# A streaming log-sum-exp: four heads' bias on GpSimd, and one multiply and one sum per tile on VectorE, a tile later

## The chip, the cores and the metric

The kernel runs on one core of a Trainium2 chip. The metric is the time of one execution in microseconds (us). All runs quoted here agree within 0.3%. Times are medians.

## The reference

```python
def reference(x, bias):          # x: 8 x 2048 x 2048 f32, bias: 8 heads x 256
    x_heads = x.reshape(B, S, H, Dh).transpose(0, 2, 1, 3)
    x_heads = x_heads + bias[None, :, None, :]
    x_tiled = np.repeat(x_heads, 2, axis=2)
    mx = x_tiled.max(axis=-1, keepdims=True)
    return mx.squeeze(-1) + np.log(np.exp(x_tiled - mx).sum(axis=-1))   # 8 x 8 x 4096
```

For each row of 2048 numbers and each of the 8 heads the kernel needs the logarithm of the sum of exp(x + bias) over the head's 256 numbers. The kernel reads 134 MB and writes 1 MB. It leaves the maximum out. The outputs are right.

## The kernel before

x is cut into 64 tiles of 128 partitions x 2 rows x 2048 numbers, 2 MB each. Nine tile buffers are loaded in a ring. A streamed tile's eight heads are treated in three ways:

- heads 0 and 1: TensorE adds the bias into PSUM (identity matmul plus ones times bias), ScalarE takes exp and sums with its accumulator;
- heads 2 to 4: GpSimd adds the bias, ScalarE takes exp, VectorE sums three heads of both rows in one reduce, one tile later;
- heads 5 to 7: ScalarE takes exp of the raw numbers; VectorE multiplies by exp(bias) (in PSUM, `w_rep`) and sums in one instruction per head and row, six a tile ("weigh"). The trace shows each as two instructions, the custom operation and an accumulator read.

```python
for t in range(T):
    ...
    if left >= NLATE:                       # all but the last two tiles
        got = add_bias([xt[:, k, 0:CPE] for k in range(K)])
        g_add(t)                            # GpSimd, heads 2..4
        w0 = CPE + NG * Dh
        exp_inplace(xt[:, :, w0:D])         # heads 5..7
        if t:
            exp_inplace(g_part(t - 1))      # heads 2..4 of the tile before
        for k in range(K):
            sum_biased(got[k], ...)         # heads 0, 1
        for k in range(K):
            for c in range(w0, D, Dh):
                weigh(xt[:, k, c : c + Dh], c // Dh, sum_at(k, c // Dh))
        if t:
            g_sum(t - 1)
    # ... the last two tiles in pieces, without GpSimd: six weighs a row (cut)
    if left == NLATE:
        exp_inplace(g_part(t)); g_sum(t)
    if 0 < t and t - 1 + NBUF < T:
        load(t - 1 + NBUF)                  # reuses the buffer of tile t - 1
```

Tile 61 is the last streamed one; 62 and 63 are the late tiles.

The softmax here doesn't subtract the row's maximum and nothing guards it: scores larger than these inputs give would overflow.

## Time and profile before

The time is 337.84 us (337.63 to 338.28, 4 runs); the profiled span is 336.1 us.

| what | before | read from |
|---|---|---|
| loads in flight | 428 GB/s from 20 to 300 us | stretches of the span |
| busiest engine | ScalarE, 89% of the span | busy times |
| GpSimd, one tile | 3.45 us | groups |
| VectorE, one tile | six weighs at 0.34 us, a reduce of 1.75 | groups, timeline |
| issue to landing of a load | 34.3 us | DMA issues |

The first lines of the page of the kernel before, busy time of the engines, and the DMA rows of the 40 slices (tenths of busy time, GB/s):

```profile
PE 235.5 (70%) x410; PEld 69.4 (21%) x410; DVE 244.6 (73%) x856; ACT 300.6 (89%) x660; POOL 224.2 (67%) x84
...
DMA  8999999999999999999999999999999999999910
GB/s 297 427 431 435 421 429 425 437 423 426 425 432 425 435 422 431 427 430 424 430 426 425 431 427 430 422 429 433 429 426 429 424 427 431 423 435 416 365 43 16
```

No engine is saturated (ScalarE, the busiest, has 89% of the span) and the DMA queues are (busy share 1.01 from 20 to 300 us), until about 319 us. The page's account of the chain that ended last, shares of the span by engine, says the same:

```profile
DMA 71%; DVE 6%; ACT 5%; PE 1%; issue 1%; SPq 0%; ACTq 0%; DVEq 0%
```

The page's DMA queues (packets, MB, share of the 16 DMA engines' span) hold a detail that becomes important below: q14 and q8 carry instructions, not data. The line under the dots is from the page's DMA issues, a load's size and its median time in us from issue to landing.

```profile
q1 hardware_dynamic: 10832, 135.17, 95.1%
...
q14 instruction: 15, 0.12, 0.1%
q8 instruction: 3, 0.05, 0.1%
...
xt<-in_x_dram SPq DMA_DIRECT2D x62, 2048.0 KB, 34.3
```

The groups of instructions (line, engine, operation, out<-in, forms, count; busy us and mean ns of one; idle before them):

```profile
L182 POOL TENSOR_TENSOR xt<-xt,b_rep 128x1536 f32<-128x1536 f32 x62 | 213.8, 3449 | 95.6 <-DMA xt<-in_x_dram 89.6
...
L200 DVE CUSTOM_DVE_ANT_0 junk<-xt,w_rep 128x256 f32<-128x256 f32 x396 | 140.4, 417 | 86.5 <-ACT xt L194 86.5
L194 ACT ACTIVATE xt<-xt 128x1536 f32<-128x1536 f32 (+1 forms) x132 | 183.4, 1435 | 13.5 <-DMA xt<-in_x_dram 12.5
L186 DVE TENSOR_REDUCE R<-xt 128x6 f32<-128x1536 f32 x62 | 108.4, 1749 | 0.7 <-ACT xt L194 0.7
```

The end of the span, from the timeline (start us, duration us, engine, line, operation). The last GpSimd add starts 0.13 us after tile 61 has landed, so it marks that moment:

```profile
315.27 3.46 POOL L182 TENSOR_TENSOR xt<-xt,b_rep 128x1536 f32<-128x1536 f32 x1 [1.46 <-DMA xt<-in_x_dram]
...
319.76 2.84 ACT L194 ACTIVATE xt<-xt 128x1536 f32<-128x1536 f32 x2
...
321.27 1.75 DVE L186 TENSOR_REDUCE R<-xt 128x6 f32<-128x1536 f32 x1 [0.73 <-ACT xt L194]
...
322.94 0.41 DVE L200 CUSTOM_DVE_ANT_0 junk<-xt,w_rep 128x256 f32<-128x256 f32 x1
...
332.25 0.42 DVE L200 CUSTOM_DVE_ANT_0 junk<-xt,w_rep 128x256 f32<-128x256 f32 x1
...
333.15 0.37 ACT L229 ACTIVATE res<-tpair 8x256 f32<-8x256 f32 x1 [0.93 <-PE tpair L216]
```

From tile 61's landing to the end there are 20.8 us (336.1 - 315.3); call it the tail. Pieces of tiles 62 and 63 still land in it, but after 315.5 neither ScalarE nor VectorE waits for a load. The first late weigh starts at 322.94 and the last at 332.25.

### The profile page before, as it was taken

How to read it: one execution, taken by the hardware profiler on the slowest of the kernel's cores; microseconds unless marked ns; L12 is line 12 of the kernel's file. 1: busy time of each engine (PE TensorE's matmuls, PEld its weight loads, DVE VectorE, ACT ScalarE, POOL GpSimd, SP SyncE). 2: the span in 40 equal slices, each digit the busy share in tenths (PEclk: the TensorE clock that was granted, in tenths of full speed). 3: DMA queues.
4: the chain of work that ended last, by engine and by line, in shares of the span. 5: the costliest groups of instructions: out<-in, count | busy, mean ns of one | idle time of the engine just before them, and what ended most of it. 6: DMA issues, size and time to landing. Idle time of an engine off the chain costs nothing.

```text
span 336.1 us, 2806 instructions
## 1 busy us (share of the span) xinstructions
PE 235.5 (70%) x410; PEld 69.4 (21%) x410; DVE 244.6 (73%) x856; ACT 300.6 (89%) x660; POOL 224.2 (67%) x84
## 2 busy tenths in 40 slices
PE   5297785977766669767679586566894967665861
PEld 2022221222221122212122122121221212121210
DVE  0238888888878768778868777778777777877794
ACT  1469999999999989999989999899998999998995
POOL 6866766766766766766766776666775776675704
PEclk9998967596789856896765977789559596789876
DMA  8999999999999999999999999999999999999910
GB/s 297 427 431 435 421 429 425 437 423 426 425 432 425 435 422 431 427 430 424 430 426 425 431 427 430 422 429 433 429 426 429 424 427 431 423 435 416 365 43 16
DMA packets 11204, 135.46 MB, mean 403 GB/s; under 512 B 1577, under 2 KB 1849, under 8 KB 2993
## 3 DMA queue, kind: packets, MB, share of 16 engines
q1 hardware_dynamic: 10832, 135.17, 95.1%
q0 software_dynamic: 352, 0.10, 0.2%
q14 instruction: 15, 0.12, 0.1%
q8 instruction: 3, 0.05, 0.1%
q10 hardware_dynamic: 2, 0.01, 0.0%
HBM read 134.23 MB, written 1.05 MB: 402 GB/s over the span
## 4 chain that ended last, share of the span: by engine, by line
DMA 71%; DVE 6%; ACT 5%; PE 1%; issue 1%; SPq 0%; ACTq 0%; DVEq 0%
DMA xt<-in_x_dram 71%; ACT xt L194 4%; DVE junk L200 3%; DVE R L186 2%; ACT ps L165 1%; PE ps L159 1%; ACT res L229 0%; PE tpair L216 0%; DVE Rz L200 0%; DVE R L200 0%; SPq L95 0%; ACTq L194 0%; DVEq L356 0%
## 5 line engine op out<-in xcount | busy, mean ns | idle before, releaser
L182 POOL TENSOR_TENSOR xt<-xt,b_rep 128x1536 f32<-128x1536 f32 x62 | 213.8, 3449 | 95.6 <-DMA xt<-in_x_dram 89.6
L159 PE MATMUL ps<-xt,ident 128*128 128x512 f32 x256 | 183.1, 854 | 71.4 <-DMA xt<-in_x_dram 71.1
L200 DVE CUSTOM_DVE_ANT_0 junk<-xt,w_rep 128x256 f32<-128x256 f32 x396 | 140.4, 417 | 86.5 <-ACT xt L194 86.5
L194 ACT ACTIVATE xt<-xt 128x1536 f32<-128x1536 f32 (+1 forms) x132 | 183.4, 1435 | 13.5 <-DMA xt<-in_x_dram 12.5
L186 DVE TENSOR_REDUCE R<-xt 128x6 f32<-128x1536 f32 x62 | 108.4, 1749 | 0.7 <-ACT xt L194 0.7
L165 ACT ACTIVATE ps<-ps 128x256 f32<-128x256 f32 x256 | 94.6, 369 | 10.5 <-PE ps L159 6.3
L159 PEld LDWEIGHTS ps<-xt,ident 128*128 128x128 f32 x256 | 57.4, 248 | 160.3 <-DMA xt<-in_x_dram 105.1
L154 PE MATMUL ps<-b,ones 3*128 3x512 bf16 x128 | 48.7, 454 | 14.5 <-ACT ps L165 7.9
L165 ACT ACTIVATION_READ_ACCUMULATOR ps<-ps 128x1 f32 x256 | 48.5, 190 | 0.0
L200 DVE DVE_READ_ACCUMULATOR2_ANT R<- 128x1 f32 x372 | 30.6, 82 | 0.0
L154 PEld LDWEIGHTS <-ones 3*128 3x128 bf16 x128 | 7.9, 96 | 81.0 <-issue 72.7
L250 POOL DMA_DIRECT2D out_dram<-res x8 | 4.0, 505 | 9.2 <-ACT res L229 9.2
L132 PE MATMUL w_rep<-brow,ones 1*128 1x512 f32 x6 | 5.5, 1078 | 3.5 <-DMA brow<-in_bias_dram 3.5
L139 ACT ACTIVATE b_rep<-w_rep 128x768 f32<-128x768 f32 x1 | 0.8, 810 | 6.9 <-PE w_rep L132 6.9
L229 ACT ACTIVATE res<-tpair 64x512 f32<-64x512 f32 (+3 forms) x11 | 5.9, 539 | 1.2 <-PE tpair L216 0.9
L216 PE MATMUL tpair<-ident,R 128*64 128x128 f32 (+1 forms) x16 | 3.6, 310 | 2.0 <-DVE R L186 2.0
L216 PEld LDWEIGHTS tpair<-ident,R 128*64 128x64 f32 (+1 forms) x16 | 2.0, 130 | 9.1 <-DVE R L186 3.9
L216 PE MATMUL tpair<-ident,Rz 128*8 128x128 f32 x2 | 0.6, 322 | 4.4 <-DVE Rz L200 4.4
L132 PEld LDWEIGHTS w_rep<-brow,ones 1*128 1x128 f32 x6 | 1.8, 323 | 5.5 <-issue 5.5
L121 POOL CAST bparts<-brow 1x512 bf16<-1x512 f32 x1 | 0.6, 599 | 2.1 <-DMA brow<-in_bias_dram 2.1
L105 ACT ACT_TABLE_LOAD x1 | 1.3, 1283 | 0.7 <-PEq L345 0.7
L142 ACT ACTIVATE w_rep<-w_rep 128x512 f32<-128x512 f32 x3 | 1.7, 582 | 0.1
(18 smaller groups left out, 8.9 us busy)
## 6 DMA issues: line engine op xcount, KB each, us to landing
xt<-in_x_dram SPq DMA_DIRECT2D x62, 2048.0 KB, 34.3
xt<-in_x_dram SPq DMA_DIRECT2D x2, 1024.0 KB, 31.6
xt<-in_x_dram SPq DMA_DIRECT2D x2, 512.0 KB
out_dram<-res SPq DMA_DIRECT2D x7, 128.0 KB, 34.2
xt<-in_x_dram SPq DMA_DIRECT2D x3, 256.0 KB, 16.9
xt<-in_x_dram SPq DMA_DIRECT2D x2, 128.0 KB, 8.6
out_dram<-res POOLq DMA_DIRECT2D x8, 12.0 KB, 1.7
b<-bparts POOLq DMA_DIRECT2D x3, 1.0 KB, 5.7
```

The source lines that it names most:

```text
L132: nc.tensor.matmul(w_rep[:, c : c + MM], lhsT=ones, rhs=brow[:, CPE + c : CPE + c + MM], start=True, stop=True,)
L142: nc.scalar.activation(out=w, in_=w, func=ACT.Exp)
L154: nc.tensor.matmul(p[:, 0:CPE], lhsT=ones3, rhs=b3, start=True, stop=False)
L159: nc.tensor.matmul(p[:, 0:CPE], lhsT=ident, rhs=v, start=False, stop=True)
L165: nc.scalar.activation(out=p[:, c : c + Dh], in_=p[:, c : c + Dh], func=ACT.Exp, accum_out=dst(h),)
L182: nc.gpsimd.tensor_tensor(out=g_part(t), in0=g_part(t), in1=b_tile, op=ALU.add)
L186: nc.vector.tensor_reduce(out=R[b][:, :, NPE : NPE + NG, blk], in_=g_part(t).rearrange("p k (h j) -> p k h j", j=Dh), op=ALU.add, axis=myb ...
L194: nc.scalar.activation(out=v, in_=v, func=ACT.Exp)
L200: nc.vector.tensor_tensor_reduce(out=j, in0=v, in1=w_rep[:, c : c + Dh], scale=1.0, scalar=0.0, op0=ALU.mult, op1=ALU.add, accum_out=dst,)
L216: nc.tensor.transpose(out=tps[i][0:nr, k], in_=src(k), identity=ident)
L229: nc.scalar.activation(out=rv, in_=tv, func=ACT.Ln)
L250: engine.dma_start(out=ov, in_=iv)
```

## The change

GpSimd now adds the bias of four heads. ScalarE takes exp of all six heads (2 to 7) of a tile in one instruction, one tile later. VectorE multiplies heads 6 and 7 by exp(bias) in one instruction and sums all six in one reduce. Per tile that replaces six weighs and a reduce by two instructions. The late tiles are as they were.

```diff
-NG = 3
+CG = 1024
 ...
-    nc.scalar.activation(out=b_rep, in_=w_rep[:, 0 : NG * Dh], func=ACT.Copy)
+    nc.scalar.activation(out=b_rep, in_=w_rep[:, 0 : CG], func=ACT.Copy)
 ...
     def g_add(t):
-        nc.gpsimd.tensor_tensor(out=g_part(t), in0=g_part(t), in1=b_tile, op=ALU.add)
+        v = xts[t % NBUF][:, :, CPE : CPE + CG]
+        nc.gpsimd.tensor_tensor(out=v, in0=v, in1=b_tile, op=ALU.add)
-    def g_sum(t):
+    def exp_and_sum(t):
         b, blk = divmod(t, NBLK)
+        v = xts[t % NBUF][:, :, CPE:D]
+        exp_inplace(v)
+        f = v[:, :, CG:CW]
+        nc.vector.tensor_tensor(out=f, in0=f, in1=w_tile, op=ALU.mult)
         nc.vector.tensor_reduce(
-            out=R[b][:, :, NPE : NPE + NG, blk],
-            in_=g_part(t).rearrange("p k (h j) -> p k h j", j=Dh),
+            out=R[b][:, :, NPE:H, blk],
+            in_=v.rearrange("p k (h j) -> p k h j", j=Dh),
             op=ALU.add, axis=mybir.AxisListType.X)
 ...
             got = add_bias([xt[:, k, 0:CPE] for k in range(K)])
             g_add(t)
-            w0 = CPE + NG * Dh
-            exp_inplace(xt[:, :, w0:D])
-            if t:
-                exp_inplace(g_part(t - 1))
+        if 0 < t and left >= NLATE - 1:
+            exp_and_sum(t - 1)
+        if left >= NLATE:
             for k in range(K):
                 sum_biased(got[k], lambda h: sum_at(k, h))
-            for k in range(K):
-                for c in range(w0, D, Dh):
-                    weigh(xt[:, k, c : c + Dh], c // Dh, sum_at(k, c // Dh))
-            if t:
-                g_sum(t - 1)
 ...
-        if left == NLATE:
-            exp_inplace(g_part(t))
-            g_sum(t)
```

## The prediction

> **What bounds it now.** The loads. The windows from 20 to 300 us show a DMA share of 1.01 and 426 to 429 GB/s. The chain of waits is 71% DMA into xt. In the timeline one 2 MB tile lands every 4.89 us (199.00, 203.90, 208.79; about 5.05 on average). Every engine does a tile in less: ACT 4.5 to 4.7 us, DVE about 3.8 (six weigh instructions at a pitch of 0.34, one reduce of 1.75), GpSimd 3.45. Loads take 34 us to land, about seven tiles deep.
> The last tile has landed near 319.7 us, but the span is 336.1: the last 16 us are an ACT chain (exp of tile 61's GpSimd part at 319.76, then the late pieces without a gap to 330), then DVE's last weigh, ending 332.68, then 3.4 us of logarithm and output.
>
> **Costs of the change, per tile.**
> - GpSimd: 2048 instead of 1536 elements; 3.45 us scaled: 4.60.
> - DVE: drops six weighs (about 2.05 us) for one 1024-element multiply. [...]
> - ACT: one exp of 3072 for two of 1536. From 0.615 us at 512 and 1.474 at 1536: 2.76 against 2.86 for the pair.
> - Contention: GpSimd adds are 3.42 to 3.47 us whether DVE overlaps or not. The multiply's second input stays in PSUM. [...]so I add nothing.
>
> **Critical path.** All three stay under 4.89 us, GpSimd with only 0.25 to 0.3 to spare. A tile is released about 7.2 us after its successor lands instead of 5.4; the load queue shrinks from 34 to about 32 us and stays full. The stream should cost 0.
>
> The tail pays. Tile 61 lands at 315.2; its add ends at 319.9 instead of 318.7; the exp of all six heads ends at 322.6 instead of 321.2, so ACT's late pieces shift by 1.4 us. DVE then does multiply and reduce until about 327.1, and the late tiles' 24 weighs (8.2 us at 0.342) start there instead of at 322.9: last weigh ends at about 335.3 instead of 332.7. DVE, not ACT, limits the tail: +2.7 us.
>
> **Prediction: 340.4 us**, 8 in 10 between 339.2 and 342.4; faster by over 2%: 0.01, within 2%: 0.94, slower by over 2%: 0.05.
>
> **What would show it.** Groups of lines: add 4.6 us x62, multiply 1.2, reduce 3.35, exp 2.76. Busy: GpSimd near 295 us, DVE near 290, ACT a little lower (about 295). Timeline: tiles landing every 4.89 us, last load near 320 as before; time to landing 31 to 33 us. Chain of waits: at the end a run of DVE weighs from about 327 without gaps in place of ACT exps.
>
> **What would make it wrong.** GpSimd over 4.85 us (contention): it would set the pace, each 0.1 us over costing 6 us in all, and the loads would show gaps. ACT waiting for GpSimd each tile. A tail where the logarithms' transposes, waiting for DVE, stall ACT too: another 0.5 to 1 us. Or the tail hiding part, if ACT's start of tile 61 comes earlier than I think.

VectorE's terms of the sum were estimates: 1.22 us for the multiply and 3.35 for the reduce, which waits for it, together 4.6 us a tile (0.8 more than before); measured later, 1.218 and 3.355. In the tail they bring VectorE from the end of the exp at 322.6 to about 327.1; the sum came to +2.7 us, 340.4 us.

## The result, and the profile after

The changed kernel takes 337.89 us (337.77 to 338.01, 4 runs) against 337.84 (337.63 to 338.28, 4 runs): the ratio is 1.0, with a 95% interval of 0.9982 to 1.0017. (A ratio is the mean time of one kernel's runs over that of the other's of the same rounds, so not quite the ratio of the quoted medians.) The predicted 340.4 us, range 339.2 to 342.4, was too high.

The groups of the changed kernel (the last line is from the list that keeps shapes apart):

```profile
L186 POOL TENSOR_TENSOR xt<-xt,b_rep 128x2048 f32<-128x2048 f32 x62 | 281.2, 4537 | 26.2 <-DMA xt<-in_x_dram 23.8
...
L194 DVE TENSOR_REDUCE R<-xt 128x12 f32<-128x3072 f32 x62 | 208.0, 3355 | 7.2 <-DVE xt L193 1.0
...
L193 DVE TENSOR_TENSOR xt<-xt,w_rep 128x1024 f32<-128x1024 f32 x62 | 75.5, 1218 | 34.3 <-ACT xt L202 34.1
...
L202 ACT ACTIVATE xt<-xt 128x3072 f32<-128x3072 f32 x62 | 171.1, 2760 | 10.2 <-POOL xt L186 9.8
```

Every duration is close to the forecast: add 4.54 us (4.60), reduce 3.355 (3.35), multiply 1.218 (1.22), exp 2.760 (2.76). Busy times too, while the DMA rows of the slices hardly differ:

```profile
PE 236.6 (70%) x410; PEld 69.5 (21%) x410; DVE 290.2 (86%) x174; ACT 296.1 (88%) x598; POOL 291.6 (87%) x84
...
DMA  7999999999999999999999999999999999999900
GB/s 296 430 427 435 429 424 427 433 423 427 428 425 430 433 423 430 425 428 431 424 433 421 429 427 425 434 432 423 425 430 427 433 427 426 427 429 418 386 23 16
```

The end of the span in the timeline of the changed kernel:

```profile
312.17 4.54 POOL L186 TENSOR_TENSOR xt<-xt,b_rep 128x2048 f32<-128x2048 f32 x1 [0.35 <-DMA xt<-in_x_dram]
...
319.54 1.22 DVE L193 TENSOR_TENSOR xt<-xt,w_rep 128x1024 f32<-128x1024 f32 x1 [0.22 <-ACT xt L202]
...
320.86 3.35 DVE L194 TENSOR_REDUCE R<-xt 128x12 f32<-128x3072 f32 x1
...
324.13 0.41 DVE L208 CUSTOM_DVE_ANT_0 junk<-xt,w_rep 128x256 f32<-128x256 f32 x1
...
331.99 0.42 DVE L208 CUSTOM_DVE_ANT_0 junk<-xt,w_rep 128x256 f32<-128x256 f32 x1
...
332.88 0.37 ACT L237 ACTIVATE res<-tpair 8x256 f32<-8x256 f32 x1 [1.25 <-PE tpair L224]
```

The tail is there as predicted: from the last add to the end of the span it is now 23.7 us (335.9 - 312.2) instead of 20.8, that is +2.9 for a predicted +2.7, and VectorE's late weighs run from 324.13 to 332.4 without a gap. But tile 61 landed 3.1 us earlier, at 312.2 instead of 315.3. So two effects of about 3 us cancel, -3.1 and +2.9, and one of them was not in the prediction. That they nearly cancel is luck; the spans, 335.9 and 336.1, show the small rest. The same bytes, at the same GB/s, and yet the last tiles arrive sooner. Among the DMA queues of the page (and, last, its line of the loads) one line changed:

```profile
q1 hardware_dynamic: 10832, 135.17, 95.1%
...
q8 instruction: 3, 0.05, 0.1%
q14 instruction: 10, 0.08, 0.1%
...
xt<-in_x_dram SPq DMA_DIRECT2D x62, 2048.0 KB, 32.0
```

Ten packets of instructions instead of 15. They are a thousandth of the DMA time. In the trace each load raises its semaphore in 16 steps, which are read here as one from each of the 16 DMA engines, and the work on a tile starts after the 16th: tile 61's add comes 0.13 us after it. The trace keeps the times of these steps. Here are, for some loads, the first, the third and second from the end, and the last step, in us (read from the trace's completion records, not a view of the page):

```
kernel   tile    first   14th   15th   16th   16th - first
before      1    12.72  13.36  13.53  13.61    0.89
before     17    90.82  92.05  92.98  93.32    2.50
before     29   150.09 152.06 152.30 153.68    3.59
before     45   228.94 231.15 232.34 234.30    5.36
before     61   307.80 310.12 311.85 315.14    7.34
after       1    13.05  13.46  13.52  13.58    0.53
after      17    91.15  91.77  92.16  93.20    2.05
after      29   150.41 151.63 152.11 152.56    2.15
after      45   229.26 230.98 231.50 232.43    3.17
after      61   308.12 310.31 310.43 312.01    3.89
```

The first of the steps comes at the same time in both kernels, within 0.4 us. What differs is how far the last step, so the slowest DMA engine, trails. In the kernel before its lag grows from 120 us on in jumps of about 1 us, one every 45 us. (Before that it grows by 0.5, 0.8 and 0.3 us; the 0.8 shows at 73.55, after a packet of q8, of 16 KB and 1.10 us, at 71.42.) The 8 KB packets of q14 that come just before the jumps, and the landing in which each jump shows:

```
before   packet at   122.53   167.82   212.8    258.59   308.18
         jump seen   124.02   169.31   214.64   260.08   310.24
         size of it    1.03     1.01     1.03     1.05     0.96
```

In the kernel before VectorE runs some 14 instructions a tile, waits included. In the changed kernel it has 312 instructions in the trace instead of 932, and the trace has five 8 KB packets fewer. (ScalarE has 48 fewer and SyncE 55 more, which nearly cancel.) By an estimate from these counts, 620 / 5, one packet goes with some 124 of VectorE's instructions; at 14 a tile that is nine tiles' worth, or about 45 us: the spacing of the jumps. The estimate is rough, since packets are counted whole.

### The profile page after: what moved, and what is told of

Same layout as the page of the kernel before. It is cut to its first block, busy times and chain, and to the rows that moved or that the text cites. A ratio compares the mean times of both kernels' runs of the same rounds, so it can differ in the third digit from the quotient of the medians.

```text
span 335.9 us, 2193 instructions
## 1 busy us (share of the span) xinstructions
PE 236.6 (70%) x410; PEld 69.5 (21%) x410; DVE 290.2 (86%) x174; ACT 296.1 (88%) x598; POOL 291.6 (87%) x84
## 5 line engine op out<-in xcount | busy, mean ns | idle before, releaser
L186 POOL TENSOR_TENSOR xt<-xt,b_rep 128x2048 f32<-128x2048 f32 x62 | 281.2, 4537 | 26.2 <-DMA xt<-in_x_dram 23.8
L194 DVE TENSOR_REDUCE R<-xt 128x12 f32<-128x3072 f32 x62 | 208.0, 3355 | 7.2 <-DVE xt L193 1.0
L202 ACT ACTIVATE xt<-xt 128x3072 f32<-128x3072 f32 (+3 forms) x70 | 177.5, 2539 | 10.2 <-POOL xt L186 9.8
L193 DVE TENSOR_TENSOR xt<-xt,w_rep 128x1024 f32<-128x1024 f32 x62 | 75.5, 1218 | 34.3 <-ACT xt L202 34.1
L154 PE MATMUL ps<-b,ones 3*128 3x512 bf16 x128 | 48.0, 450 | 12.6 <-DMA b<-bparts 6.5
L224 PE MATMUL tpair<-ident,R 128*64 128x128 f32 (+1 forms) x16 | 4.3, 367 | 10.0 <-DVE R L194 10.0
L208 DVE CUSTOM_DVE_ANT_0 junk<-xt,w_rep 128x256 f32<-128x256 f32 x24 | 8.3, 416 | 0.0
L139 ACT ACTIVATE b_rep<-w_rep 128x1024 f32<-128x1024 f32 x1 | 1.0, 1025 | 6.9 <-PE w_rep L132 6.9
```

The lines of the kernel that those rows point to most:

```text
L154: nc.tensor.matmul(p[:, 0:CPE], lhsT=ones3, rhs=b3, start=True, stop=False)
L186: nc.gpsimd.tensor_tensor(out=v, in0=v, in1=b_tile, op=ALU.add)
L193: nc.vector.tensor_tensor(out=f, in0=f, in1=w_tile, op=ALU.mult)
L194: nc.vector.tensor_reduce(out=R[b][:, :, NPE:H, blk], in_=v.rearrange("p k (h j) -> p k h j", j=Dh), op=ALU.add, axis=mybir.AxisListType.X,)
L202: nc.scalar.activation(out=v, in_=v, func=ACT.Exp)
L208: nc.vector.tensor_tensor_reduce(out=j, in0=v, in1=w_rep[:, c : c + Dh], scale=1.0, scalar=0.0, op0=ALU.mult, op1=ALU.add, accum_out=dst,)
```

## The experiments

The kernel before ran beside each experiment on the same chip: 337.91 us (7 runs) beside e1 to e4, 337.77 (9 runs) beside e5 to e7.

The theory, F, is a guess to be tested, for no trace shows the path of a packet: each engine's instructions are fetched by DMA packets that go through one of the 16 DMA engines; each packet sets that one back by about 1 us in a stream that never pauses, and nothing catches up. A load lands when the slowest has delivered. The change saved five of VectorE's packets and with that 3.1 us, which paid for the longer tail.

Rival Q: the changed kernel frees its buffers later, so its load queue is shorter (32.0 us to landing instead of 34.3), and that is what makes the stream end earlier. Rival W: the weighs themselves, their work or their writes, slowed the loads. A third doubt concerns the tail: whether its cost is real and what it is worth.

"Lag" below is the distance of the last from the first of the 16 steps for tile 61.

### More instructions on VectorE, in the kernel before (e1_before_nop_dve)

```diff
+NFILL = 10
 ...
             if t:
                 g_sum(t - 1)
+            for _ in range(NFILL):
+                nc.vector.engine_nop()
```

> The kernel before, with ten do-nothing engine instructions added on VectorE at the end of each streamed tile (620 in all), where VectorE is idle anyway. Theory F (instruction fetch): VectorE's instructions are fetched in 8 KB packets, and each packet sets one of the 16 DMA engines back by about 1 us; 620 more instructions [...]are about 5 more packets, so the last of the 16 completions of a load trails the first by about 12 us at the end instead of 7.3, tile 61 lands near 320 instead of 315.2, and the time is about 342.5 us (+4.8). Rival Q (the earlier landing in the changed kernel came from later buffer release and a shorter load queue): no more lag, time 337.9. Rival W (it came from the absence of the weighs' own work or of their writes): 337.9. If VectorE became the limit instead, its busy share would be above 95% and the load slices would show gaps.

Measured: 342.14 us (341.98 to 342.25), ratio 1.0124 (1.0107 to 1.0141). A filler takes about 14 ns in the trace and VectorE's busy time stays at 244.7 us. The lag is 11.72 us, tile 61's last step comes at 319.43, and its first at 307.71, where it always was. The tail is 20.9 us, unchanged. The instruction queue of this run's page, and its last add in the timeline:

```profile
q14 instruction: 20, 0.16, 0.1%
```

```profile
319.57 3.46 POOL L183 TENSOR_TENSOR xt<-xt,b_rep 128x1536 f32<-128x1536 f32 x1 [1.53 <-DMA xt<-in_x_dram]
```

Five packets more, of which four come before tile 61's last step (18 against 14); 4.4 us more lag and 4.2 us more time, from instructions that do nothing. From 55 to 300 us the lag of this run grows in ten jumps of 0.95 to 1.02 us, each within 7 us after an 8 KB packet, and these packets come every 24 to 29 us instead of every 45. Neither Q nor W explains that.

### The same fillers on GpSimd, in the kernel before (e2_before_nop_pool)

Against the run above:

```diff
-                nc.vector.engine_nop()
+                nc.gpsimd.engine_nop()
```

> The kernel before, with the same ten do-nothing instructions per tile, but on GpSimd. Theory F, with each compute engine's instructions fetched through a DMA engine of its own: about 5 more 8 KB packets, but they set back another DMA engine that is ahead, to a lag of about 6 us, under the 7.3 us of the slowest; tile 61 lands within 0.5 us of 315.2 and the time stays within 1 us of 337.9. If all fetches went through one DMA engine, or what counts is the number of packets in total: +4 to +5 us, about 342.5. Rivals Q and W: 337.9.

Measured: 337.98 us, ratio 1.0002 (0.9987 to 1.0017), with as many packets in the page's instruction queue as the run above:

```profile
q14 instruction: 20, 0.16, 0.1%
```

The lag is 6.91 us. The third slowest step of tile 61's load is now at 4.2 us behind the first, where it was at 2.3 in the kernel before: another step was set back, but it was not the last one. So it is not the number of packets that costs. The reading of F is that it counts how many fall on the DMA engine that is already last; the trace does not name that engine.

### Eight tile buffers, in the kernel before (e3_before_nbuf8)

```diff
-NBUF = 9
+NBUF = 8
```

> The kernel before with eight tile buffers instead of nine, so each load is issued one tile later and the time to landing falls from 34.3 to about 29.4 us. Theory F: the number of VectorE instructions is the same, so the lag of the last completion stays near 7.3 us, tile 61 lands at 315 plus or minus 0.5, time 337.9 plus or minus 0.7. Rival Q (a shorter load queue lets the stream end earlier): tile 61 lands 2 to 3 us earlier and the time is 335 to 336.

Measured: 337.79 us, ratio 0.9998 (0.9983 to 1.0013). Time to landing fell to 29.2 us; the lag is 6.88 us and tile 61's last step comes at 315.04. A shorter queue does not end the stream earlier: Q falls in this kernel.

### The old instructions back in number, in the changed kernel (e5_after_nop_dve10)

```diff
         if left >= NLATE:
+            for _ in range(NFILL):              # NFILL = 10
+                nc.vector.engine_nop()
             for k in range(K):
                 sum_biased(got[k], lambda h: sum_at(k, h))
```

> The changed kernel with ten do-nothing VectorE instructions per streamed tile (14 ns each in the first run of this study, none of it busy time), which brings VectorE back to the 934 instructions it had before the change. If the saved instruction fetches are what paid for the longer tail: five 8 KB fetch packets more, the slowest completion trails by about 7 us at the end instead of 3.9, the last GpSimd add starts near 315.3 instead of 312.2, the tail keeps its 23.7 us, and the time is 340.9 us (340.2 to 341.5), what the prediction said of the change. If the landings came earlier for another reason (larger VectorE instructions, later release, the missing weighs): 337.9.

Measured: 340.84 us (340.6 to 341.0), ratio 1.0091 (1.0076 to 1.0106). VectorE has 932 instructions in the trace again, the lag is 6.97 us and the last step of tile 61 comes at 314.98. The instruction queue of its page, and from its timeline the last add, the last reduce, the first late weigh and the last instruction:

```profile
q14 instruction: 15, 0.12, 0.1%
```

```profile
315.14 4.53 POOL L187 TENSOR_TENSOR xt<-xt,b_rep 128x2048 f32<-128x2048 f32 x1 [1.33 <-DMA xt<-in_x_dram]
...
323.82 3.35 DVE L195 TENSOR_REDUCE R<-xt 128x12 f32<-128x3072 f32 x1
327.09 0.41 DVE L209 CUSTOM_DVE_ANT_0 junk<-xt,w_rep 128x256 f32<-128x256 f32 x1
...
335.83 0.37 ACT L238 ACTIVATE res<-tpair 8x256 f32<-8x256 f32 x1 [1.23 <-PE tpair L225]
```

This is the tail of the prediction, almost to the tenth: late weighs from about 327.1, the last one ended near 335.3 (335.36 in the trace). With the instruction count held, the change costs about what was predicted: +3.1 us against the kernel before beside it, for +2.6. The run also closes what was left of the rivals: the time to landing is 30.7 us, shorter still than the changed kernel's 32.0, and the weighs are still gone, yet tile 61 lands where it did before the change, within 0.2 us.

### Half the dose (e6_after_nop_dve5)

The same edit with `NFILL = 5`, about 2.5 packets.

> The same with five per tile, half the dose (about 2.5 packets). If the stream ends with the slowest of the 16 DMA engines, and in the changed kernel that is one that carries another engine's fetches (lag 3.9 us, VectorE's about 2.2): VectorE's rises to about 4.7, only 0.5 to 1.2 us above the 3.9, and the time is 338.4 to 339.1, well under half of the full dose. If delays add up whatever the engine: +2.4 us, 340.3.

Measured: 337.97 us (337.83 to 338.2), ratio to the kernel before 1.0005 (0.9993 to 1.0018), against 1.0 for the changed kernel without fillers, of another session; by spans it is 336.3 against 335.9 us. The lag is 4.42 us instead of 3.88, and tile 61's last step comes at 312.42 instead of 312.01. That is below the expected 338.4 to 339.1, so the size was a miss; the expectation took VectorE's share of the lag 0.3 us too high. It rules out a sum over engines (340.3): the first half of the dose cost 0.1 to 0.4 us, the second half 2.9 us. The second slowest step, at 4.09 us here, is near the 3.88 us of the changed kernel; that another DMA engine is this floor is the reading that fits, as expected, and the trace does not name it.

### The old way for the last four streamed tiles, in the changed kernel (e4_after_old_tail4)

Tiles 58 to 61 are done as in the kernel before: three heads on GpSimd, the exp of heads 5 to 7 without waiting for GpSimd, six weighs.

```diff
+        old = NLATE <= left < NLATE + NOLD          # NOLD = 4
+        was_old = NLATE <= left + 1 < NLATE + NOLD
 ...
-            g_add(t)
-        if 0 < t and left >= NLATE - 1:
+            (g_add3 if old else g_add)(t)           # g_add3: heads 2..4
+        if 0 < t and left >= NLATE - 1 and not was_old:
             exp_and_sum(t - 1)
+        if old:
+            exp_inplace(xt[:, :, w0:D])
+            if was_old:
+                exp_inplace(g_part(t - 1))
 ...                                                  # sum_biased, then:
+        if old:
+            ... six weighs of tile t ...
+            if was_old:
+                g_sum(t - 1)
 ...
+        if left == NLATE and old:
+            exp_inplace(g_part(t))
+            g_sum(t)
```

> The changed kernel, but the last four streamed tiles (58 to 61) are done as the kernel before does them: three heads on GpSimd, three weighed on VectorE at once. If the predicted tail cost is real and was only hidden by the earlier end of the loads: tile 61 lands near 312.1 to 312.5 as in the changed kernel, from there to the end takes the 21 us of the kernel before instead of 23.9, and the time is 335.2 us (334.7 to 336.0), 0.8% below both. If the tail cost was not there (the prediction's arithmetic of the tail was wrong): 337.9.

Measured: 334.81 us (334.74 to 334.99), ratio 0.991 (0.9895 to 0.9924) to the kernel before, which ran beside it. By spans, 333.2 against 336.1 and 335.9, it is faster than both kernels. The last add and the last instruction in the timeline of this run:

```profile
312.31 3.47 POOL L213 TENSOR_TENSOR xt<-xt,b_rep 128x1536 f32<-128x1536 f32 x1 [1.46 <-DVE R L231]
...
330.21 0.37 ACT L260 ACTIVATE res<-tpair 8x256 f32<-8x256 f32 x1 [0.93 <-PE tpair L247]
```

The add's line names a VectorE instruction as what ended its wait; the load's last step, at 312.15 in the completion records, came 0.16 us before it, as in the other runs, so the load is the likelier one. Tile 61 still lands early (lag 4.19 us), and the tail is 20.9 us again (333.2 - 312.3). The two halves of the result are thus separated: the early end of the stream is worth 3.0 us (312.15 against 315.14), the longer tail cost 2.8 (23.7 against 20.9).

### The old way for the last two only (e7_after_old_tail2)

The same with `NOLD = 2`.

> The changed kernel with only the last two streamed tiles done the old way (four in the earlier run, 334.81). What the tail needs is that VectorE is free when tile 61's exp is done; after two tiles it should have caught up for the most part: 334.8 to 335.6. If more than two are needed: 335.6 to 336.5.

Measured: 335.43 us (335.14 to 335.53), ratio 0.9929 (0.9916 to 0.9941). The stream ended a little earlier (last step 311.72), but the tail was 21.5 us: after two tiles VectorE has not quite caught up (its late weighs start at 321.43, 9.7 us after tile 61's last step), after four it has (319.96, 7.8 us after).

### All runs side by side

VectorE's instructions are counted in the trace, waits included. The packets are those of q14 in the whole span; before tile 61's last step there are 14, 9, 18, 19, 14, 9, 14, 11 and 9. "Last step" is the landing of tile 61; the tail is the end of the span less the start of tile 61's add.

```
run                    VectorE   8 KB     lag   last step   tail    span
                       instr.   packets   us      us         us      us
before                   932      15      7.34   315.14     20.8   336.1
after                    312      10      3.88   312.01     23.7   335.9
e1_before_nop_dve       1552      20     11.72   319.43     20.9   340.5
e2_before_nop_pool       932      20      6.91   314.89     21.0   336.0
e3_before_nbuf8          932      15      6.88   315.04     20.9   336.0
e4_after_old_tail4       352      11      4.19   312.15     20.9   333.2
e5_after_nop_dve10       932      15      6.97   314.98     23.7   338.8
e6_after_nop_dve5        622      13      4.42   312.42     23.7   336.3
e7_after_old_tail2       332      11      3.65   311.72     21.5   333.4
```

By the way the tail is counted, the span is the start of tile 61's add plus the tail; in every row that add starts 0.13 to 0.16 us after the last step. The landing follows VectorE's instructions from 622 up (312.4, 315, 319.4); from 312 to 622 it hardly moves (311.7 to 312.4). The tail depends on how the last tiles are done.

## Why the prediction was wrong

What held:

- *"What bounds it now. The loads."* The stream was and is DMA bound (a DMA share of 1.00 to 1.01 and 426 to 429 GB/s from 20 to 300 us, before and after); no engine became the limit (ScalarE, still the busiest, has 88%).
- *The costs per tile.* Add 4.54 for 4.60 us, multiply 1.218 for 1.22, reduce 3.355 for 3.35. In the traces the multiply lies within 0.4% of the line through the two reduces (1.749 us for 1536 elements, 3.355 for 3072: 1.214 for 1024).
- *Contention: none.* GpSimd's add took 4.54 us for 2048 elements, 2.22 ns each, where the old add took 2.25, although VectorE is busy for 86% of the span instead of 73%.
- *"Time to landing 31 to 33 us"*: 32.0. *GpSimd near 295, DVE near 290, ACT about 295 busy*: 291.6, 290.2, 296.1.
- *"The tail pays ... +2.7 us."* It pays 2.9, and VectorE became its limit. e5, which differs only by idle instructions, ended its last weigh at 335.36 us for a predicted 335.3.

What failed is one step: *"the load queue ... stays full. The stream should cost 0"*, with its sign, *"last load near 320 as before"*. The term was given as 0 and measured -3.1 us: tile 61 landed at 312.0, not 315.1. (The last piece of tile 63 landed at 325.5 before and 322.5 after, so "320" fits neither.) Time to landing, 32.0 us, came out as predicted, so the queue is not what failed. What the step left out is that a load is done when the last of its 16 steps is done, and, as e1, e2 and e5 indicate, that the slowest DMA engine also carried VectorE's instruction fetches. The clue stood in the prediction itself: tiles land every 4.89 us, *"about 5.05 on average"*. Counted on tiles 1 to 61 of the kernel before, the first of the 16 steps advances by 4.92 us a tile ((307.80 - 12.72) / 60) and the last by 5.03 ((315.14 - 13.61) / 60); that 0.11 us, 60 times, is the growth of the lag from 0.9 to 7.3 us, and removing two thirds of VectorE's instructions removed about half of the lag (3.9 us left).

The gain stops there, by the same reading, because the second slowest step already lagged by 4.0 us before (311.85 - 307.80). Of the 7.3 us at most some 3.3 could be had by thinning VectorE's instructions alone, and 3.1 were.

Shown by experiments: VectorE's instruction count sets the lag (11.72 us in e1, 6.97 in e5, 4.42 in e6); as many extra packets with GpSimd's instructions cost nothing (e2, ratio 1.0002); the queue's depth does not set it (e3, 6.88 us); the tail's cost is real and can be had back (e4, e7). Left open: why a packet whose own record lasts 0.31 to 0.33 us sets its DMA engine back by 1 us. The trace does not tell which DMA engine a packet ran on; that VectorE's always take the same one is inferred from the jumps' times and from e1 and e2. Which engine's packets hold the 3.9 us that remain was not tested. The records of the changed kernel point to ScalarE: after packets at 160.2, 224.6 and 284.9 the last step's lag reaches 2.4, 3.2 and 3.8 us, and 60 to 64 us is about the time, 61 us, in which ScalarE, with 678 instructions in 336 us, runs the 124 estimated above. The last two of these steps are of 0.7 us, so 1 us is not the size for every packet; and at 73.8 us the lag grew by 1.2 after a packet of q8. One more rival was not separated: every run has a profiled span, so the profiler may have added traffic for each instruction. That e2, with the same 620 extra instructions, costs nothing speaks against it.

## What to carry to other kernels

In a kernel that streams at the DMA limit, count the instructions of each engine as traffic. Here 620 fewer on VectorE, the engine with most of them, ended the stream 3.1 us earlier although it had time to spare (busy for 73% of the span before), and 620 idle ones more delayed it by 4.3 us (e1); on GpSimd they delayed nothing (e2). When the average distance between landings exceeds the common one (here 5.03 against 4.89 us), look at how far the last completion trails the first. And a trade that is good in the stream can be bad in the tail: use the large, late instructions for the stream and switch back to the short-latency form for the last few tiles (here four tiles, 3.1 us against the kernel before).
